# Values of a hybrid decoder layer formed by channels and turned by TensorE, in place of values formed by tokens

## The chip, the cores and the metric

The kernel runs on one core of one Trainium2 chip. The metric is device time in microseconds (us) of one execution. The engines are named as in the profile: PE (TensorE, matmuls; PEld its weight loads), DVE (VectorE), ACT (ScalarE), POOL (GpSimd), SP (which issues the DMAs).

## The reference

One decoder layer over 1024 tokens of width 1024, all in float32: an RMS norm, one combined input projection, three mixers side by side (a gated linear recurrence HGRN2 with 4 heads of 128, a sparse attention over the best 256 keys of each query, a cross-attention to 256 memory tokens), an output projection with residual, and a SwiGLU feed-forward part with residual.

```python
h = rmsnorm(x, norm_mix[layer])
hq, hf, hi, hg, sq, sk, sv, iq, ik, iw, mq = split_in(h @ w_in[layer])
o_hg = hgrn2_mix(hq, hf, hi, hg, lb[layer], hg_out_gain[layer])
o_sa = dsa_mix(sq, sk, sv, iq, ik, iw, sa_q_gain[layer], sa_k_gain[layer])
o_mem = mem_mix(mq, mem_n, w_mem_kv[layer], ...)
x = x + concat([o_hg, o_sa, o_mem]) @ w_out[layer]
a, b = split(rmsnorm(x, norm_ffn[layer]) @ w_ffn_in[layer])
x = x + (silu(a) * b) @ w_ffn_out[layer]
```

The change concerns `hi` (1024 tokens x 512, the values of the four HGRN2 heads) and `sv` (1024 x 256, the values of the sparse attention). Both are used with tokens on the partitions.

## The kernel before, in words

The normed tokens lie transposed, channels on partitions: `H[p][k][hf]` is the high (p = 0) or low (p = 1) part of channels 128k to 128k + 127 of token half `hf` (512 tokens), not yet scaled by the tokens' RMS factor. Each fp32 product is made in three passes over high and low parts (`PASSES`). The factor is applied later: `rn` holds it with tokens on partitions, `rrow` as a row over the tokens.

Most projections (`proj`, line 186) hold a 128x128 block of weights stationary and move 512 tokens; the result has channels on partitions and goes through a PSUM bank of tag `mm`. Each PSUM tag has two banks. The values need tokens on partitions, so `token_major` (lines 447 to 461) holds a block of 128 tokens stationary and moves 256 weight columns: 8 token tiles x 2 halves of the contraction x 12 matmuls (L457) into four banks (`lg`, `lg`, `sm`, `sm`), two token tiles a bank. `scaled_rows` (L463 to L467) copies them out on ACT, scaled by `rn` (8 copies, L466). There are three calls: `hgrn_v(0)` (heads 0 and 1), `sparse_values`, `hgrn_v(1)` (heads 2 and 3).

Around them run, interleaved on the engines:

- two searches for the 256th best score (`bisect`, L622): 31 bits each, one count of all keys per bit. The V search (blocks 7 and 4) counts on DVE (L646). The S search (blocks 6, 5, 3, 2) counts on ACT (L643, four counts a bit) and steps on DVE (L648, L655, L658, L638). Behind the search, the masks of the four blocks are made one by one: L668 counts, then for each block L678 on DVE, L680 on POOL, L683, L684 and L685 on DVE, L686 on POOL.
- the recurrence of each head: the projections and gates (L485, L497 to L506, sigmoids on ACT), then `hgrn_intra`: a descent over widths w = 1, 2, 4 to 64, in which PE forms products (L518, L553) and `descend` multiplies Q on DVE (L527), K on POOL (L528) and the decay on DVE (L529). `hgrn_state` then transposes the descended K (L571, copied by ACT, L572) and forms the states (L578, L594, L596). Nothing of L571 needs the values; L578 does.
- the memory attention (L697 to L724; exponentials on ACT, L704), the sparse queries and keys, and the loading and splitting of weight pages (L117 on ACT, L118 on POOL).

Every engine executes its instructions in order. That order is not the program's: the framework plans it, with its own model of times, and with tile releases placed by it, so that a change in one place moves instructions elsewhere. Once planned it is fixed.

Of the kernel before, what the change touches and what calls it, by code (L numbers as in the profile page):

```python
# [15 lines left out]
AF = mybir.ActivationFunctionType  # L16
# [26 lines left out]
def hybrid_block(ctx, tc, xT, memT, wch, wikw, wv, wkm, wvm, woa, wob, wfi, wfo,  # L43
                 vec, cst, lvl, out):
    nc = tc.nc
    V, S, G, T = nc.vector, nc.scalar, nc.gpsimd, nc.tensor
# [17 lines left out]
    def tmp(n=512):  # L64
        return tp.tile([128, n], F32, tag="tmp", name=nm("tmp"))

    def bank(tag):

        return pp.tile([128, 512], F32, tag=tag, name=nm(tag))
# [10 lines left out]
    def hs(hf):  # L80
        return slice(hf * 512, hf * 512 + 512)

    def bs(b):
        return slice(b * 128, b * 128 + 128)
# [23 lines left out]
    ident = cs[:, C_ID:C_ID + 128]  # L108
# [29 lines left out]
    PASSES = ((0, 0), (0, 1), (1, 0))  # L138
# [305 lines left out]
    Vh = [None] * 4  # L444
    heads = {}

    def token_major(g0):

        acc = [bank("lg"), bank("lg"), bank("sm"), bank("sm")]
        for g in range(2):  # L450
            w = load_page(wv[g0 + g], 4, 256)
            for tt in range(8):
                o = acc[tt // 2][:, 256 * (tt % 2):256 * (tt % 2) + 256]
                i = 0
                for pw, p in PASSES:
                    for k in range(4):
                        T.matmul(o, H[p][4 * g + k][tt // 4][:, bs(tt % 4)], w(pw, k),  # L457
                                 start=g == 0 and i == 0 and tt % 2 == 0,
                                 stop=g == 1 and i == 11 and tt % 2 == 1)
                        i += 1  # L460
        return [a.rearrange("p (t d) -> p t d", t=2) for a in acc]

    def scaled_rows(dst, acc):  # L463

        for tt in range(8):
            S.activation(dst[tt // 4][:, tt % 4, :], acc[tt // 2][:, tt % 2, :], AF.Copy,  # L466
                         scale=rn[:, tt:tt + 1])  # L467

    def hgrn_v(pair):
        ph[0] = "hg"  # L470
        Vp = [xt(10 + j, [128, 4, 256]) if pair else mt(4 + j, (128, 4, 256)) for j in range(2)]
        scaled_rows(Vp, token_major(2 * pair))
        for j in range(2):
            Vh[2 * pair + j] = lambda c, j=j: Vp[c // 4][:, c % 4, bs(j)]

# [273 lines left out]
    def sparse_values():  # L749
        ph[0] = "sap"  # L750
        sv.extend((xt(6, [128, 4, 256]), xt(7, [128, 4, 256])))
        scaled_rows(sv, token_major(4))

    def sparse_queries():
        ph[0] = "sap"
# [604 lines left out]
```

## Time and profile before

| | us |
|---|---|
| median of 3 executions (lowest, highest) | 1390.32 (1389.21, 1392.29) |
| the profiled execution | 1390.27 |
| its span | 1388.5 |
| PE, DVE, ACT, POOL busy | 1302.4, 1056.7, 692.0, 475.1 |

The span is the time between the first and the last recorded instruction; the profiled execution's own time is 1.8 us longer. A busy time counts an engine's instructions, whether or not anything waits for them, and an average over the span says nothing of a stage: the windows and the chain of waits show which engine ends last where. The feed-forward part, from about 560 us on, is untouched by the change.

### The profile page before, as it was taken

To read this page: it belongs to the slowest core of one execution; us is meant where nothing else is said; L and a number is where in the kernel's file an instruction comes from. 1 tells how busy PE (TensorE), PEld (TensorE's weight loads), DVE (VectorE), ACT (ScalarE), POOL (GpSimd) and SP (SyncE) were. 2 spreads that over 40 slices of the span, in tenths; PEclk is the share of its full clock that TensorE was granted. 3 is DMA by queue.
4 is the path that set the end of the run, shared out by engine and by line. 5 is a ranking of instruction groups with operands and counts; after the bars stand their busy time and mean duration, and the time that the engine had idled before them with its cause. 6 is when DMAs were issued, how large, how long until landed. Compare 5 with 4: busy or idle time off the path is not lost.

```text
span 1388.5 us, 22035 instructions
## 1 busy us (share of the span) xinstructions
PE 1302.4 (94%) x8072; PEld 1066.3 (77%) x8072; DVE 1056.7 (76%) x2094; ACT 692.0 (50%) x1369; POOL 475.1 (34%) x395
## 2 busy tenths in 40 slices
PE   7989999988989995999997999999999998999998
PEld 4767787668878884776885888888888886878887
DVE  8696998896469689775678787777787766696764
ACT  7555879956853243656454333333333334334442
POOL 2311033355257633424005233232332210384520
PEclk9999999999999996899998999999999999999999
DMA  6210010000010001013331322223223219754241
GB/s 236 69 39 16 28 50 16 32 32 32 31 48 31 26 26 46 2 61 125 125 108 61 114 99 105 93 92 113 99 99 107 91 54 346 238 185 154 84 145 61
DMA packets 53244, 122.19 MB, mean 88 GB/s; under 512 B 6032, under 2 KB 6160, under 8 KB 53136
## 3 DMA queue, kind: packets, MB, share of 16 engines
q1 hardware_dynamic: 52848, 120.58, 25.2%
q8 instruction: 63, 1.03, 0.3%
q14 instruction: 45, 0.37, 0.1%
q10 hardware_dynamic: 288, 0.22, 0.1%
HBM read 92.19 MB, written 28.57 MB: 87 GB/s over the span
## 4 chain that ended last, share of the span: by engine, by line
PE 59%; DVE 6%; POOL 2%; ACT 2%; issue 2%; DMA 1%; ACTq 0%; DVEq 0%; POOLq 0%
PE ff_lg L1093 17%; PE ff_rc L1093 12%; PE fo_mm L1252 4%; PE fo_sm L1252 4%; PE wo_mm L1052 3%; PE fo_lg L1252 2%; PE fo_rc L1252 2%; PE wo_sm L1052 2%; PE sap_mm L186 2%; PE hg_mm L186 2%; PE sat_sm L856 1%; PE sat_lg L830 1%; PE wo_mm L186 1%; PE sat_mm L875 1%; PE sat_rc L875 1%
## 5 line engine op out<-in xcount | busy, mean ns | idle before, releaser
L117 ACT ACTIVATE ff_whi<-ff_x 128x512 fp32r<-128x512 f32 x112 | 70.0, 629 | 125.4 <-PE ff_rc L1093 70.1
L643 ACT ACTIVATE idx_x<-idx_x,packs 128x896 int8<-128x896 f32 (+3 forms) x128 | 105.7, 826 | 41.6 <-DVE packs L638 34.9
L1093 PE MATMUL ff_lg<-wo_h,ff_whi 128*128 128x512 f32 x396 | 104.8, 391 | 2.8 <-ACT wo_h L117 2.8
L186 PE MATMUL hg_mm<-xn_h,hg_whi 128*128 128x512 f32 x384 | 96.9, 395 | 0.0
L1093 PE MATMUL ff_rc<-wo_h,ff_whi 128*128 128x512 f32 x308 | 90.5, 393 | 0.6 <-DVE wo_h L177 0.6
L1093 PE MATMUL ff_lg<-wo_x,ff_whi 128*128 128x512 f32 x308 | 84.9, 404 | 5.3 <-ACT ff_tmp L1100 4.8
L1093 PEld LDWEIGHTS ff_lg<-wo_h,ff_whi 128*128 128x128 f32 x396 | 74.6, 188 | 18.7 <-ACT wo_h L117 3.3
L118 DVE TENSOR_TENSOR ff_wlo<-ff_x,ff_whi 128x512 fp32r<-128x512 f32 x112 | 82.1, 741 | 8.7 <-ACT ff_whi L117 4.0
L186 PEld LDWEIGHTS hg_mm<-xn_h,hg_whi 128*128 128x128 f32 x384 | 70.5, 188 | 14.5 <-issue 0.7
L118 POOL TENSOR_TENSOR hg_wlo<-hg_wst,hg_whi 128x512 fp32r<-128x512 f32 x32 | 43.0, 1356 | 104.9 <-ACT hg_whi L117 79.4
L1093 PEld LDWEIGHTS ff_lg<-wo_x,ff_whi 128*128 128x128 f32 x308 | 57.6, 192 | 24.0 <-ACT ff_whi L117 7.3
L646 DVE TENSOR_SCALAR_CACHE_REDUCE idx_x<-idx_x,packs 128x1024 int8<-128x1024 f32 x64 | 68.7, 1074 | 0.9
L1093 PEld LDWEIGHTS ff_rc<-wo_h,ff_whi 128*128 128x128 f32 x308 | 58.6, 190 | 13.6 <-DVE wo_h L177 1.4
L1093 PE MATMUL ff_rc<-wo_x,ff_whi 128*128 128x512 f32 x220 | 64.3, 389 | 0.0
L1030 POOL TENSOR_TENSOR ff_x<-ff_wst 128x512 f32<-128x512 f32 x7 | 13.4, 1911 | 134.6 <-PE wo_sm L1052 71.3
L528 POOL TENSOR_TENSOR hg_x<-hg_x,hg_x 128x256 f32<-128x256 f32 x56 | 49.4, 898 | 29.0 <-PE hg_rc L518 18.7
L1093 PE MATMUL ff_lg<-wo_h,ff_wlo 128*128 128x512 f32 x198 | 55.8, 390 | 0.0
L388 DVE SCALAR_TENSOR_TENSOR idx_x<-idx_tmp,packs,idx_x 128x512 f32<-128x512 f32 (+2 forms) x70 | 46.1, 710 | 12.2 <-ACT idx_tmp L383 11.9
L118 DVE TENSOR_TENSOR fo_wlo<-fo_tmp,fo_whi 128x512 fp32r<-128x512 f32 x33 | 33.2, 1006 | 27.0 <-ACT fo_whi L117 27.0
L186 PE MATMUL hg_mm<-xn_h,hg_wlo 128*128 128x512 f32 x192 | 50.9, 397 | 0.0
L1093 PEld LDWEIGHTS ff_rc<-wo_x,ff_whi 128*128 128x128 f32 x220 | 41.3, 188 | 8.6
L118 DVE TENSOR_TENSOR fo_wlo<-fo_h,fo_whi 128x512 fp32r<-128x512 f32 x31 | 33.5, 1081 | 18.1 <-ACT fo_whi L117 18.0
(484 smaller groups left out, 3697.5 us busy)
## 6 DMA issues: line engine op xcount, KB each, us to landing
gd<-ff_m SPq DMA_DIRECT2D x77, 256.0 KB, 2.0
fo_x<-gd SPq DMA_DIRECT2D x77, 256.0 KB, 4.0
ff_x<-wfi SPq DMA_DIRECT2D x16, 512.0 KB, 3.4
ff_wst<-wfi SPq DMA_DIRECT2D x14, 512.0 KB, 3.3
ff_m<-wfi SPq DMA_DIRECT2D x14, 512.0 KB, 3.2
hg_wst<-wch SPq DMA_DIRECT2D x12, 512.0 KB, 3.3
fo_x<-wfo SPq DMA_DIRECT2D x24, 256.0 KB, 5.2
fo_h<-wfo SPq DMA_DIRECT2D x20, 256.0 KB, 4.4
```

The source lines that it names most:

```text
L117: S.activation(hi, src, AF.Copy)
L118: (eng or V).tensor_sub(lo, src, hi.bitcast(F32))
L186: T.matmul(ps[:M, :], w(pw, k), h[p][k][hf], start=i == 0, stop=i == len(order) - 1)
L388: V.scalar_tensor_tensor(sc[b][:, c0:c1], rl[:, :c1 - c0], iww[:, b, h:h + 1], sc[b][:, c0:c1], op0=ALU.mult, op1=ALU.add)
L528: G.tensor_mul(Kv[:, :, 0, :], Kv[:, :, 0, :], fr.to_broadcast([128, n, w]))
L643: S.activation(waste[S][:, :nk], sc[b], AF.Sign, bias=nf[:, j:j + 1], accum_out=ct[:, j:j + 1])
L646: eng.tensor_scalar(waste[eng][:, :nk], sc[b], fl[:, j:j + 1], None, op0=ALU.is_ge, op1=ALU.add, accum_out=ct[:, j:j + 1])
L830: T.matmul(lg[:, :c1 - c0], qst[h][b // 4][:, bs(b % 4)], kst[h][p][c][:, :c1 - c0], start=p == 0, stop=p == 1)
L875: T.matmul(po[ROWS[j], 0:128], sv[kb // 4][:, kb % 4, 128 * m + 64 * j:128 * m + 64 * j + 64], PTs[j][:, kb, :], start=kb == 0, stop=kb == ...
L1052: mm = T.matmul(ps, lhs, rhs, start=i == 0, stop=i == len(steps) - 1)
L1093: mm = T.matmul(ps, w[pw][:, bs(k)], HB[u][k][p], start=first and i == 0, stop=i == 11, skip_group_check=True)
L1252: T.matmul(banks[m], w[i][pw][:, bs(m)], b[i][p], start=first and i == 0 and n == 0, stop=i == NP - 1 and n == 2, skip_group_check=True)
```

## The change

`token_major` and `scaled_rows` go; `values(g0, dst)` takes their place in all three calls. It holds 128 weight columns stationary and moves 512 tokens: 2 contraction halves x 2 column blocks j x 2 token halves hf x 12 matmuls (in the new file still L457) into four banks of the same tags. The result has channels on partitions. Then for each of the four banks DVE multiplies it by `rrow` into an SBUF tile (L463), PE transposes four 128x128 blocks into a bank of tag `mm` (L466), and ACT copies that bank to its place (L467). The values end up where they were.

```diff
--- before.py
+++ after.py
@@ -444,32 +444,32 @@
     Vh = [None] * 4
     heads = {}
 
-    def token_major(g0):
-
-        acc = [bank("lg"), bank("lg"), bank("sm"), bank("sm")]
+    def values(g0, dst):
+
+        acc = [[bank(t), bank(t)] for t in ("lg", "sm")]
         for g in range(2):
             w = load_page(wv[g0 + g], 4, 256)
-            for tt in range(8):
-                o = acc[tt // 2][:, 256 * (tt % 2):256 * (tt % 2) + 256]
-                i = 0
-                for pw, p in PASSES:
-                    for k in range(4):
-                        T.matmul(o, H[p][4 * g + k][tt // 4][:, bs(tt % 4)], w(pw, k),
-                                 start=g == 0 and i == 0 and tt % 2 == 0,
-                                 stop=g == 1 and i == 11 and tt % 2 == 1)
-                        i += 1
-        return [a.rearrange("p (t d) -> p t d", t=2) for a in acc]
-
-    def scaled_rows(dst, acc):
-
-        for tt in range(8):
-            S.activation(dst[tt // 4][:, tt % 4, :], acc[tt // 2][:, tt % 2, :], AF.Copy,
-                         scale=rn[:, tt:tt + 1])
+            for j in range(2):
+                for hf in range(2):
+                    i = 0
+                    for pw, p in PASSES:
+                        for k in range(4):
+                            T.matmul(acc[j][hf], w(pw, k)[:, bs(j)], H[p][4 * g + k][hf],
+                                     start=g == 0 and i == 0, stop=g == 1 and i == 11)
+                            i += 1
+        for j in range(2):
+            for hf in range(2):
+                t = tmp()
+                V.tensor_mul(t, acc[j][hf], rrow[:, hs(hf)])
+                tb = bank("mm")
+                for c in range(4):
+                    T.transpose(tb[:, bs(c)], t[:, bs(c)], ident)
+                S.activation(dst[hf][:, :, bs(j)], tb.rearrange("p (a b) -> p a b", a=4), AF.Copy)
 
     def hgrn_v(pair):
         ph[0] = "hg"
         Vp = [xt(10 + j, [128, 4, 256]) if pair else mt(4 + j, (128, 4, 256)) for j in range(2)]
-        scaled_rows(Vp, token_major(2 * pair))
+        values(2 * pair, Vp)
         for j in range(2):
             Vh[2 * pair + j] = lambda c, j=j: Vp[c // 4][:, c % 4, bs(j)]
 
@@ -749,7 +749,7 @@
     def sparse_values():
         ph[0] = "sap"
         sv.extend((xt(6, [128, 4, 256]), xt(7, [128, 4, 256])))
-        scaled_rows(sv, token_major(4))
+        values(4, sv)
 
     def sparse_queries():
         ph[0] = "sap"
```

The plan of every engine's order changes with it. Three places follow; in the rows, out<-in name tiles, the numbers are the tiles' own, and `waits` names the engine (or DMA queue) whose signal an instruction waits for.

First place, behind the S search, DVE: before, from the first w = 64 multiplication (L527 of shape 128x4x64) of head 1's descent on.

```order
L527 TENSOR_TENSOR hg_x_499_2775<-hg_x_499_2775,hg_x_501_2777 128x4x64 [waits PE_49]
L678 TENSOR_SCALAR idx_x_156_809,packs<-idx_x_158_811,packs 128x512 [waits DVE_49]
L527 TENSOR_TENSOR hg_x_499_2775<-hg_x_499_2775,hg_x_501_2777 128x4x64 [waits PE_49]
L529 TENSOR_TENSOR hg_x_501_2777<-hg_x_501_2777 128x4 [waits DVE_49]
L681 TENSOR_SCALAR packs<-packs 128x1 [waits DVE_49]
L683 SCALAR_TENSOR_TENSOR idx_x_158_811<-idx_x_158_811 128x512 [waits Pool_49]
L529 TENSOR_TENSOR hg_x_501_2777<-hg_x_501_2777 128x4 [waits DVE_49]
L684 SCALAR_TENSOR_TENSOR idx_x_158_811<-idx_x_158_811,packs 128x512 [waits DVE_49]
L561 COPY hg_tot_3844<-hg_x_501_2777 128x8 [waits DVE_49]
L685 SCALAR_TENSOR_TENSOR idx_x_158_811<-idx_x_156_809,idx_x_158_811 128x512 [waits DVE_49]
L678 TENSOR_SCALAR idx_x_156_809,packs<-idx_x_157_810,packs 128x384 [waits DVE_49]
```

The two w = 64 multiplications stand around L678 of the third block, ahead of its L683. After the change, from the third block's L684 on:

```order
L684 SCALAR_TENSOR_TENSOR idx_x_158_811<-idx_x_158_811,packs 128x512 [waits DVE_49]
L527 TENSOR_TENSOR hg_x_507_2703<-hg_x_507_2703,hg_x_509_2705 128x8x32 [waits PE_49] x2
L685 SCALAR_TENSOR_TENSOR idx_x_158_811<-idx_x_156_809,idx_x_158_811 128x512 [waits DVE_49]
L529 TENSOR_TENSOR hg_x_509_2705<-hg_x_509_2705 128x8 [waits DVE_49] x2
L678 TENSOR_SCALAR idx_x_156_809,packs<-idx_x_157_810,packs 128x384 [waits DVE_49]
L681 TENSOR_SCALAR packs<-packs 128x1 [waits DVE_49]
L683 SCALAR_TENSOR_TENSOR idx_x_157_810<-idx_x_158_811 128x384 [waits Pool_49]
L684 SCALAR_TENSOR_TENSOR idx_x_157_810<-idx_x_157_810,packs,idx_x_158_811 128x384 [waits DVE_49]
L685 SCALAR_TENSOR_TENSOR idx_x_157_810<-idx_x_156_809,idx_x_157_810 128x384 [waits DVE_49]
L527 TENSOR_TENSOR hg_x_507_2703<-hg_x_507_2703,hg_x_509_2705 128x4x64 [waits PE_49] x2
L529 TENSOR_TENSOR hg_x_509_2705<-hg_x_509_2705 128x4 [waits DVE_49] x2
L561 COPY hg_tot_3700<-hg_x_509_2705 128x8 [waits DVE_49]
```

The w = 32 pair now comes behind L684 of the third block, the w = 64 pair behind L685 of the fourth.

The same place on POOL, before, from the third block's L680 on (idx_x is a block's scores, hg_wlo a weight page's low part):

```order
L680 TENSOR_SCALAR idx_x_158_811<-idx_x_158_811,packs 128x512 [waits DVE_49,Pool_49]
L118 TENSOR_TENSOR hg_wlo_4527<-hg_wst_4524,hg_whi_4526 128x512 [waits DMAHW1_49,PE_49,Activation_49]
L118 TENSOR_TENSOR hg_wlo_4531<-hg_wst_4524,hg_whi_4530 128x512 [waits PE_49,Activation_49]
L528 TENSOR_TENSOR hg_x_500_2776<-hg_x_500_2776,hg_x_501_2777 128x4x64 [waits PE_49,Pool_49]
L686 TENSOR_SCALAR idx_x_156_809<-idx_x_156_809 128x768 [waits DVE_49]
L528 TENSOR_TENSOR hg_x_500_2776<-hg_x_500_2776,hg_x_501_2777 128x4x64 [waits PE_49,Pool_49]
L680 TENSOR_SCALAR idx_x_158_811<-idx_x_157_810,packs 128x384 [waits DVE_49,Pool_49]
```

and after the change, from the same L680 on:

```order
L680 TENSOR_SCALAR idx_x_158_811<-idx_x_158_811,packs 128x512 [waits DVE_49,Pool_49]
L686 TENSOR_SCALAR idx_x_156_809<-idx_x_156_809 128x768 [waits DVE_49]
L528 TENSOR_TENSOR hg_x_508_2704<-hg_x_508_2704,hg_x_509_2705 128x8x32 [waits PE_49] x2
L680 TENSOR_SCALAR idx_x_158_811<-idx_x_157_810,packs 128x384 [waits DVE_49,Pool_49]
L686 TENSOR_SCALAR idx_x_158_811<-idx_x_158_811 128x512 [waits DVE_49]
L118 TENSOR_TENSOR hg_wlo_4373<-hg_wst_4370,hg_whi_4372 128x512 [waits DMAHW2_49,PE_49,Activation_49]
L686 TENSOR_SCALAR idx_x_157_810<-idx_x_157_810 128x384 [waits DVE_49]
L118 TENSOR_TENSOR hg_wlo_4377<-hg_wst_4370,hg_whi_4376 128x512 [waits PE_49,Activation_49]
L528 TENSOR_TENSOR hg_x_508_2704<-hg_x_508_2704,hg_x_509_2705 128x4x64 [waits PE_49,Pool_49] x2
```

The last w = 64 instruction of POOL (L528, 128x4x64) stood ahead of the fourth L680; now the pair stands behind the fourth L680, behind L686 of the last two blocks and behind another weight split.

Second place, PE at the transposes of head 1's K (L571, 128x128), before:

```order
L186 MATMUL hg_mm_4498<-xn_h_176,hg_whi_4468 128x512
L571 MATMUL hg_rc_4073<-packs,hg_x_500_2776 128x128 [waits Pool_49]
L571 MATMUL hg_rc_4073<-packs,hg_x_500_2776 128x128 x3
L186 MATMUL hg_mm_4498<-xn_h_180,hg_whi_4468 128x512
L186 MATMUL hg_mm_4498<-xn_h_184,hg_whi_4468 128x512
L571 MATMUL hg_rc_4079<-packs,hg_x_500_2776 128x128 [waits Pool_49]
L571 MATMUL hg_rc_4079<-packs,hg_x_500_2776 128x128 x3
L186 MATMUL hg_mm_4498<-xn_h_188,hg_whi_4468 128x512
L186 MATMUL hg_mm_4498<-xn_h_159,hg_wlo_4465 128x512
```

and after:

```order
L186 MATMUL hg_mm_4282<-xn_h_187,hg_wlo_4253 128x512
L553 MATMUL hg_rc_3684<-hg_x_507_2703,hg_x_508_2704 64x64 [waits DVE_49,Pool_49]
L553 MATMUL hg_rc_3684<-hg_x_507_2703,hg_x_508_2704 64x64 x3
L553 MATMUL hg_rc_3684<-hg_x_507_2703,hg_x_508_2704 64x64 [waits DVE_49,Pool_49]
L553 MATMUL hg_rc_3684<-hg_x_507_2703,hg_x_508_2704 64x64 x3
L571 MATMUL hg_rc_3857<-packs,hg_x_508_2704 128x128 [waits Activation_49,Pool_49]
L571 MATMUL hg_rc_3857<-packs,hg_x_508_2704 128x128 x3
L571 MATMUL hg_rc_3863<-packs,hg_x_508_2704 128x128 [waits Activation_49,Pool_49]
L571 MATMUL hg_rc_3863<-packs,hg_x_508_2704 128x128 x3
```

Projection matmuls (L186) stood between and behind the transposes, 39 of a pair of 48 ahead of the last four; now all 48 are done before the w = 64 products (L553), and the transposes follow these at once.

Third place, ACT in the S search, where sigmoids (L499, L500) and exponentials (L704) alternate: before,

```order
L499 ACT_TABLE_LOAD
L499 ACTIVATE hg_x_465_2284<-hg_x_466_2285 128x512
L500 ACTIVATE hg_x_466_2285<-hg_x_466_2285 128x512
L643 ACTIVATE idx_x_158_811,packs<-idx_x_155_808,packs 128x896
L643 ACTIVATE idx_x_158_811,packs<-idx_x_156_809,packs 128x768
L724 ACTIVATE mat_m_365_1631<-mat_sm_2017 128x128
L643 ACTIVATE idx_x_158_811,packs<-idx_x_158_811,packs 128x512
L715 ACTIVATE mat_m_383_1866<-mat_rc_2037 128x512
L704 ACT_TABLE_LOAD
```

and after:

```order
L704 ACT_TABLE_LOAD
L704 ACTIVATE mat_m_390_1793,mat_sm_2009<-mat_lg_2003,mat_mx_2008,packs 128x256 x2
L500 ACT_TABLE_LOAD
L500 ACTIVATE hg_x_474_2213<-hg_x_474_2213 128x512
L643 ACTIVATE idx_x_158_811,packs<-idx_x_155_808,packs 128x896
L643 ACTIVATE idx_x_158_811,packs<-idx_x_156_809,packs 128x768
L643 ACTIVATE idx_x_158_811,packs<-idx_x_158_811,packs 128x512
L724 ACTIVATE mat_m_364_1630<-mat_sm_1971 128x128
L643 ACTIVATE idx_x_158_811,packs<-idx_x_157_810,packs 128x384
L704 ACT_TABLE_LOAD
L704 ACTIVATE mat_m_390_1793,mat_sm_2035<-mat_lg_2029,mat_mx_2034,packs 128x256 x2
```

The sigmoids L499 and L500 of one half stood behind one table load; now exponentials come between them and each needs a load. In the whole program there are four more table loads than before, all four among the counts of the S search.

## Rows read from the trace of the kernel before

**Rows 1.** The page, section 1: busy time of each engine, share of the span, instructions.
```profile
PE 1302.4 (94%) x8072; PEld 1066.3 (77%) x8072; DVE 1056.7 (76%) x2094; ACT 692.0 (50%) x1369; POOL 475.1 (34%) x395
```

**Rows 2.** Chain that ended last, 380 to 520: start, length (us), what.
```profile
414.11 2.54 POOL idx_x L680
...
436.06 1.02 POOL hg_x L528
437.13 0.66 PE hg_rc L571 x4
...
439.85 1.56 PE hg_rc L578 x14
...
444.76 10.90 PE hg_mm L186 x48
455.66 0.88 PE hg_rc L612 x8
...
505.17 3.46 PE sap_mm L186 x15
508.73 0.68 DVE sap_h L811
```

**Rows 3.** Timeline of DVE: the last count of the S search taken up.
```profile
405.91 0.17 DVE L648 TENSOR_TENSOR packs<-packs 128x4 int32<-128x4 f32 x1 [1.82 <-ACT idx_x L643]
```

**Rows 4.** Waits, 154 to 406: engine, line, what released it, total us, times, longest.
```profile
DVE packs L648 <- ACT idx_x L643: 38.6, 16, 5.0
...
ACT idx_x L643 <- DVE packs L638: 34.9, 21, 6.0
```

**Rows 5.** Windows: us; busy of PE, PEld, DVE, ACT, POOL; clock; DMA.
```profile
154.00:214.00 60.00, 59.79 (x390) 52.77 (x388) 58.34 (x180) 47.82 (x114) 14.02 (x16) 1.00 0.11 36
214.00:275.00 61.00, 56.58 (x336) 43.39 (x337) 51.35 (x152) 56.54 (x131) 24.41 (x36) 1.00 0.08 27
...
414.10:437.10 23.00, 21.19 (x170) 18.59 (x168) 22.37 (x33) 7.62 (x17) 22.38 (x17) 1.00 0.11 40
...
304.00:308.00 4.00, 3.38 (x12) 3.10 (x13) 3.96 (x14) 2.26 (x6) 1.32 (x1) 0.50 0.00 0
...
441.00:508.70 67.70, 67.70 (x751) 56.46 (x750) 49.43 (x138) 20.68 (x38) 29.59 (x32) 1.00 0.11 34
508.70:558.00 49.30, 32.02 (x473) 26.26 (x471) 47.73 (x123) 20.07 (x33) 20.06 (x17) 0.69 0.10 33
```

**Rows 6.** Groups by line and form, DVE, 140 to 440: total us, mean ns.
```profile
L485 DVE TENSOR_TENSOR hg_x<-hg_mm,rrow 128x512 f32<-128x512 f32 x12 | 8.2, 682 | 1.1 <-PE hg_mm L186 1.1
```

**Rows 7.** Groups by line and form, ACT, 140 to 440.
```profile
L704 ACT ACT_TABLE_LOAD x4 | 5.1, 1283 | 0.1
...
L572 ACT ACTIVATE hg_x<-hg_rc 128x512 f32<-128x512 f32 x4 | 2.4, 588 | 0.7 <-POOL hg_x L528 0.6
...
L466 ACT ACTIVATE hg_m<-hg_lg,packs 128x256 f32<-128x256 f32 x4 | 1.7, 464 | 0.0
```

**Rows 8.** Timeline of PE in the first call: start, length (us), what.
```profile
151.70 1.12 PE L457 MATMUL hg_lg<-hg_whi,xn_h 128*128 128x256 f32 x8
152.66 0.64 PE L457 MATMUL hg_lg<-hg_wlo,xn_h 128*128 128x256 f32 x4
153.14 1.12 PE L457 MATMUL hg_lg<-hg_whi,xn_h 128*128 128x256 f32 x8
```

**Rows 9.** Timeline of POOL behind the S search.
```profile
423.95 2.66 POOL L528 TENSOR_TENSOR hg_x<-hg_x,hg_x 128x256 f32<-128x256 f32 x2
...
430.70 3.45 POOL L118 TENSOR_TENSOR hg_wlo<-hg_wst,hg_whi 128x512 fp32r<-128x512 f32 x2
...
437.06 1.24 POOL L680 TENSOR_SCALAR idx_x<-idx_x,packs 128x384 int8<-128x384 f32 x1
438.38 1.33 POOL L686 TENSOR_SCALAR idx_x<-idx_x 128x512 f32<-128x512 f32 x1
```

**Rows 10.** Waits of PE, 150 to 440, the longest kind.
```profile
PE hg_rc L518 <- DVE hg_x L527: 6.2, 6, 3.4
```

## The prediction

> **What bounds the kernel now.** I read the page first: TensorE (PE) is busy 94% of a span of 1388.5 us [rows 1], which says that most of the program is paced by matmuls but not which part of it the three changed calls lie in. So the second view is the chain of waits: from 441 us to 508.7 it is PE without a gap, then DVE (the split of the sparse keys, L811), later PE again to the end [rows 2]. Just ahead of that the chain leaves PE: it goes back over the last diagonal transposes L571, a POOL product L528 and the POOL masks L680 to the instant at which DVE takes up the last count of the S search, L648 at 405.91 [rows 2, 3]. I call that instant E. All three calls (150 to 188, 312 to 353, 388 to 424 us) lie before it or just behind it, so two questions decide: when does E come, and how long is it from E to the continuous PE stretch.
>
> Third, the waits: before E, DVE waits 38.6 us for the ACT counts, ACT waits 34.9 us for the DVE steps [rows 4]. The search is thus a ping-pong of ACT and DVE, and PE only matters to it indirectly. Fourth, the windows: in 154 to 214 DVE is busy 58.34 of 60 us, in 214 to 275 ACT 56.54 of 61; from 414.1 to 437.1 DVE 22.37 and POOL 22.38 of 23; in 441 to 508.7 PE 67.70 of 67.70; behind that DVE 47.73 of 49.3 [rows 5]. What is lost before 441 is therefore passed on: the PE stretch behind it has no idle time to give back.
>
> All sums are made against the profiled execution, 1390.27 us, which is the median of the runs shown (1390.32) within 0.05.
>
> **The change part by part.**
>
> *PE.* A call had 192 matmuls with 256 moving columns, 12 in 1.44 us (151.70 to 153.14) [rows 8], 0.120 us each, so 23.0 us. Now it has 96 with 512; the projection of the same shape runs 48 in 10.90 us [rows 2], 0.227 each, so 21.8. The 16 transposes are priced by L612, the same 128x128 form, 8 in 0.88 us [rows 2]: 1.76 a call. Net +0.56 us a call, 1.7 in all. Before E PE has waits of its own (the longest kind alone 6.2 us [rows 10]) and I take 0; the bounds are 0 and +1.7. Halving the weight loads buys nothing by itself: they go with the matmuls, and the rows price both together.
>
> The Trainium skill ("TensorE: Matmul & The Clock Gate", Part 4: PE-mode transpose) speaks against this change more strongly: it gives about 275 ns for a 128x128 transpose inside a kernel. By that figure 16 would be 4.4 us a call and the net +3.2 a call, 9.6 in three; the trace's 110 ns per transpose is what I use.
>
> *DVE.* Twelve multiplies of 128x512 out of PSUM are new; L485 is the same operation, 682 ns [rows 6]. The four of the first call, 2.7 us, come into the stretch where DVE is busy 58.34 of 60 [rows 5] and the search's own steps queue behind them: +2.7 on E. The four of the second call come where DVE waits for ACT [rows 4]: 0. The four of the third lie behind E, beside POOL's masks: 0 of their own, since POOL is the pacer there (below). Bounds for all twelve: 0 and +8.2.
>
> *ACT.* 24 copies of 128x256 at 464 ns go, 12 of 128x512 at 588 ns come [rows 7]: 11.1 less 7.1, a gain of 4.1 us. But the new order has four more table loads, 1283 ns each [rows 7], all in the part of the S search where sigmoids (L499, L500) and the exponentials of the memory attention (L704) alternate among its counts: +5.1. Of the copies, 16 gone and 8 new lie before E (7.4 and 4.7), so the net on ACT before E is +2.4. ACT waits 34.9 us for DVE in that span [rows 4], but only 4.5 of it lie in 214 to 275 [rows 5]. I take 0, since DVE is the one I have lengthened already; bounds 0 and +5.1.
>
> On the trace these loads have 0.1 us of idle time before four of them [rows 7], so their price is 1.28 each. The Trainium skill ("ScalarE: Activation LUTs", What ACT_TABLE_LOAD costs) adds a drain and puts a switch at about 2.66 us. By that the four loads would be 10.6 us instead of 5.1; no row here shows such a gap.
>
> *The order behind E*, the largest term. Before, head 1's last two descents (w = 32 and 64: L527 on DVE, L528 on POOL) were spread among the masks of the four blocks, and the last L528 ended at 437.07, 31.2 us after E [rows 2, 3]. Now DVE does its w = 64 pair only after L685 of the fourth block, and POOL its w = 64 pair after every L680 and L686. POOL was busy 22.38 of the 23.0 us from its first mask to that last L528 [rows 5], so whatever is put ahead of the last L528 delays it. That is one more pair L528 (w = 8, 2.66), one more pair L118 (3.45), the fourth L680 (1.24), L686 of the third block (1.33) [rows 9] and of the fourth (scaled from the third by its width, an estimate of 1.0): 9.7 us. Behind it PE saves something: before, 9 projection matmuls stood between L571 and L578, which began 2.72 us after L571 [rows 2]; now they are done earlier, and L578 waits only for the L571 pair and two copies L572 (0.3 + 0.1 + 2 x 0.588 [rows 7], say 1.6), 1.1 less. So +8.6 from E to the state of PE at L578, and PE then idles some 6 us before L571. Bounds: 0 (if POOL's instructions run shorter with DVE less busy beside them, or PE is late itself) and +9.7 plus what the clock takes: where PE starved at about 300 us the granted clock was 0.50 in the next 4 us [rows 5], at most 2 us lost; so +11.7.
>
> *Nothing else.* SP issues the same transfers, and up to the output projection in the same order, so no transfer is added or moved past another in the part that counts.
>
> Sum: 0 + 2.7 + 0 + 8.6 = +11.3, so **1401.6 us**.
>
> **The rivals.** A difference of 0.2% (2.8 us) is about what a measurement of this kernel can tell from no change.
>
> *Faster: the calls are shorter where they count.* PE has no idle time to speak of in 154 to 214 (59.79 of 60 [rows 5]). If matmul progress sets that part, the 23.0 against 21.8 us counts with 1.2 us in each of three calls, the transposes fall into PE's waits, ACT's lighter copies before E give another 2.7, and the masks hide the late L528: 1390.3 - 3.6 - 2.7 = 1384.0. Against it: the search waits for ACT and DVE, never for PE [rows 4], and POOL behind E is full. It decides if E comes before 403. By the Trainium skill ("TensorE: Matmul & The Clock Gate", Back-to-back issue gap) a sustained stream with 512 columns runs at 131 ns a matmul, which would make this rival much stronger (12.6 us a call); the projections here, at 227, disagree.
>
> *No difference: the order behind E costs nothing.* If POOL waited on DVE rather than set the pace from 414 to 437 (DVE is as busy, 22.37 [rows 5]), the late w = 64 pair may come with the fourth mask only a little later than before, and the first call's 2.7 us may fit into the 1.7 us that DVE has free in 154 to 214: 1390 to 1392.
>
> *Slower still: table loads and bank waits.* ACT is the fuller engine from 214 to 275. If the four loads stand on the ping-pong there, E moves 5.1 more: 1401.6 + 5.1 = 1406.7. The transposes write to the two banks that projections use; where PE stands at one until a multiply is done, one multiply a group is the price, 0.7 us, so up to 2.7 in a call.
>
> **How the numbers follow.** The forecast (E later by some us, L571 some 8 later behind it) 0.60; slower still 0.14; no difference 0.12; faster 0.14. So slower by over 0.2%: 0.74, within 0.2%: 0.12, faster: 0.14. The whole order before E is planned anew and can move E by a few us either way without any of these terms. The range runs from 1388 (the forecast's tail cut to nothing and half the gain of the first rival's copies) to 1408 (slower still with some waits at banks); the forecast's own range is 1394 to 1407. What it leaves out are the fast rival and the far side of the slow one, about 2 in 10.
>
> **What would show it.** In the profile after: 12 in 2.72 us for L457, 110 ns for each transpose, 682 for L463, 588 for L467; 15 or 16 table loads; the last L648 of the S search at 407 to 411 instead of 405.91; a wait of PE at L571 on POOL L528 of about 6 us; L578 some 41 us after E instead of 33.9; then again about 67.7 us of PE without a gap. I am wrong if E is not later than 406, if L571 has no wait, or if the stretch behind 441 is shorter than before by as much as the stretch ahead of it is longer.

## The result and the profile after

The change makes the kernel slower: 1399.64 us (median of 4 executions, 1397.66 to 1401.30) against 1391.30 for the kernel before on the same chip, a ratio of 1.0061 (95% interval 1.0045 to 1.0077), +8.3 us by the medians. The forecast was 1401.6, +11.3. The profiled execution took 1398.90 us with a span of 1397.1.

The page's first section, beside [rows 1]:

```profile
PE 1309.1 (94%) x7832; PEld 1061.0 (76%) x7832; DVE 1063.5 (76%) x2106; ACT 695.4 (50%) x1361; POOL 473.5 (34%) x395
```

PE is busy 6.7 us more and DVE 6.8; the span grew by 8.6. The average says no more than that. The chain that ended last, beside [rows 2] (start, length, what):

```profile
444.12 0.59 POOL hg_x L528
...
444.76 1.97 PE hg_rc L571 x8
446.73 2.48 PE hg_rc L578 x14
...
452.56 10.93 PE hg_mm L186 x48
463.49 0.88 PE hg_rc L612 x8
...
512.95 3.46 PE sap_mm L186 x15
...
516.50 0.68 DVE sap_h L811
```

and on DVE's timeline the last count of the S search, beside [rows 3], the instant E:

```profile
405.18 0.14 DVE L648 TENSOR_TENSOR packs<-packs 128x4 int32<-128x4 f32 x1
```

E is at 405.18, not later than before (405.91): the search takes 0.8 us longer and begins 1.5 us earlier. From E to the first transpose L571 it is 39.6 us (before 29.7), to L578 41.6 (before 33.9), to the first L612 58.3 (before 49.8). From L612 on, both kernels need the same: the projection that ends in DVE's L811 takes 3.46 us in both, and from L612 to the end of the span it is 933.6 us against 932.8. So the whole loss lies between E and L612. The waits (engine, line, releaser: us, times, longest), of PE in 150 to 450 us and of DVE and ACT in 154 to 415, beside [rows 4, 10]:

```profile
PE hg_rc L571 <- POOL hg_x L528: 6.1, 1, 6.1
PE hg_mm L466 <- DVE hg_tmp L463: 4.0, 3, 1.4
```

```profile
DVE packs L648 <- ACT idx_x L643: 19.4, 12, 4.1
...
DVE hg_x L485 <- PE hg_mm L186: 8.1, 4, 2.6
DVE hg_m L485 <- PE hg_mm L186: 4.2, 2, 2.2
```

```profile
ACT idx_x L643 <- DVE packs L638: 20.0, 13, 3.0
```

PE stands 6.1 us at L571 and waits for POOL's L528. POOL's timeline shows what came ahead of that instruction, beside [rows 9]:

```profile
420.95 2.20 POOL L680 TENSOR_SCALAR idx_x<-idx_x,packs 128x768 int8<-128x768 f32 x1 [2.18 <-DVE hg_x L529]
...
435.01 1.73 POOL L528 TENSOR_TENSOR hg_x<-hg_x,hg_x 128x256 f32<-128x256 f32 x2
436.72 1.93 POOL L680 TENSOR_SCALAR idx_x<-idx_x,packs 128x384 int8<-128x384 f32 x1
438.73 1.36 POOL L686 TENSOR_SCALAR idx_x<-idx_x 128x512 f32<-128x512 f32 x1
440.17 1.44 POOL L118 TENSOR_TENSOR hg_wlo<-hg_wst,hg_whi 128x512 fp32r<-128x512 f32 x1
442.12 0.61 POOL L686 TENSOR_SCALAR idx_x<-idx_x 128x384 f32<-128x384 f32 x1 [0.51 <-DVE idx_x L685]
442.81 1.31 POOL L118 TENSOR_TENSOR hg_wlo<-hg_wst,hg_whi 128x512 fp32r<-128x512 f32 x1
444.09 1.20 POOL L528 TENSOR_TENSOR hg_x<-hg_x,hg_x 128x256 f32<-128x256 f32 x2
```

Between the w = 32 pair (435.01) and the w = 64 pair (444.09) stand the fourth L680, the last two L686 and two weight splits, as the plan had it. The windows (us; busy of PE, PEld, DVE, ACT, POOL; granted clock; DMA), beside [rows 5]:

```profile
154.00:214.00 60.00, 58.59 (x321) 49.19 (x320) 58.44 (x182) 46.47 (x110) 14.85 (x18) 1.00 0.11 36
214.00:275.00 61.00, 54.36 (x313) 42.41 (x311) 48.33 (x146) 57.77 (x125) 22.48 (x32) 0.94 0.08 27
414.10:437.10 23.00, 19.42 (x174) 15.47 (x174) 21.56 (x33) 6.81 (x13) 20.22 (x17) 0.93 0.08 24
440.00:442.00 2.00, 0.00 (x0) 0.00 (x0) 1.97 (x3) 0.00 (x0) 1.53 (x2) 0.86 0.00 0
442.00:444.00 2.00, 0.00 (x0) 0.00 (x0) 2.00 (x4) 0.00 (x0) 1.80 (x2) 0.50 0.00 0
444.00:446.00 2.00, 1.24 (x6) 1.24 (x7) 0.70 (x3) 0.04 (x1) 1.28 (x3) 0.50 0.43 102
446.00:448.00 2.00, 2.00 (x10) 1.72 (x9) 0.00 (x0) 1.16 (x2) 0.00 (x0) 0.50 0.43 168
448.00:450.00 2.00, 2.00 (x19) 2.00 (x18) 1.25 (x4) 0.00 (x0) 0.00 (x0) 0.94 0.00 0
452.60:516.40 63.80, 63.80 (x716) 52.64 (x715) 46.60 (x130) 20.00 (x37) 26.76 (x29) 1.00 0.10 29
```

PE does nothing from 440 to 444. Its granted clock is then 0.50, the lower level of 1.2 GHz, from 442 to 448, and so the 14 matmuls L578 take 2.48 us in place of 1.56. From 452.6 on PE is busy without a gap, as it was before. The rows of prices, beside [rows 6 to 8]: PE's value matmuls, DVE's multiplies, ACT's copies and table loads.

```profile
408.27 1.98 PE L457 MATMUL hg_lg<-xn_h,hg_whi 128*128 128x512 f32 x8
410.08 1.07 PE L457 MATMUL hg_lg<-xn_h,hg_wlo 128*128 128x512 f32 x4
410.99 1.98 PE L457 MATMUL hg_sm<-xn_h,hg_whi 128*128 128x512 f32 x8
```

```profile
L704 ACT ACT_TABLE_LOAD x6 | 7.7, 1283 | 0.1
...
L463 DVE TENSOR_TENSOR hg_tmp<-hg_lg,rrow 128x512 f32<-128x512 f32 x4 | 2.7, 686 | 0.0
...
L467 ACT ACTIVATE hg_m<-hg_mm 128x512 f32<-128x512 f32 x4 | 2.2, 598 | 1.4 <-PE hg_mm L466 1.4
```

Twelve matmuls take 2.72 us (408.27 to 410.99), 227 ns each; a multiply 686 ns, a copy 598.

### The profile page after: what moved, and what is told of

It reads as the page before. It is cut to its first block, busy times and chain, and to the rows that moved or that the text cites. A ratio compares the mean times of both kernels' runs of the same rounds, so it can differ in the third digit from the quotient of the medians.

```text
span 1397.1 us, 21562 instructions
## 1 busy us (share of the span) xinstructions
PE 1309.1 (94%) x7832; PEld 1061.0 (76%) x7832; DVE 1063.5 (76%) x2106; ACT 695.4 (50%) x1361; POOL 473.5 (34%) x395
## 4 chain that ended last, share of the span: by engine, by line
PE 59%; DVE 5%; ACT 2%; issue 1%; DMA 1%; POOL 0%; ACTq 0%; DVEq 0%; POOLq 0%
PE ff_lg L1093 17%; PE ff_rc L1093 12%; PE fo_mm L1252 4%; PE fo_sm L1252 4%; PE wo_mm L1052 3%; PE fo_rc L1252 3%; PE fo_lg L1252 3%; PE wo_sm L1052 2%; PE sap_mm L186 2%; PE hg_mm L186 2%; PE sat_sm L856 1%; PE sat_lg L830 1%; PE wo_mm L186 1%; PE sat_rc L875 1%; PE sat_mm L875 1%
## 5 line engine op out<-in xcount | busy, mean ns | idle before, releaser
L186 PE MATMUL hg_mm<-xn_h,hg_whi 128*128 128x512 f32 x384 | 102.2, 410 | 0.0
L186 PEld LDWEIGHTS hg_mm<-xn_h,hg_whi 128*128 128x128 f32 x384 | 73.2, 196 | 14.8 <-issue 0.3
L118 POOL TENSOR_TENSOR hg_wlo<-hg_wst,hg_whi 128x512 fp32r<-128x512 f32 x32 | 41.6, 1314 | 108.9 <-ACT hg_whi L117 66.9
L528 POOL TENSOR_TENSOR hg_x<-hg_x,hg_x 128x256 f32<-128x256 f32 x56 | 49.6, 904 | 30.4 <-PE hg_rc L518 24.5
L186 PE MATMUL hg_mm<-xn_h,hg_wlo 128*128 128x512 f32 x192 | 52.0, 404 | 0.0
L1093 PE MATMUL ff_rc<-wo_h,ff_wlo 128*128 128x512 f32 x154 | 46.5, 395 | 0.0
```

The lines of the kernel that those rows point to most:

```text
L118: (eng or V).tensor_sub(lo, src, hi.bitcast(F32))
L186: T.matmul(ps[:M, :], w(pw, k), h[p][k][hf], start=i == 0, stop=i == len(order) - 1)
L528: G.tensor_mul(Kv[:, :, 0, :], Kv[:, :, 0, :], fr.to_broadcast([128, n, w]))
L1093: mm = T.matmul(ps, w[pw][:, bs(k)], HB[u][k][p], start=first and i == 0, stop=i == 11, skip_group_check=True)
```

## The experiments

Each kernel was timed in five rounds against the kernel before on the same chip. Besides the time, three stages of its profiled execution are given: the S search (from the first count on ACT to E), E to L571 and E to the first L612. They can be told apart because the edits leave the plan ahead of E as it is in the kernel that they start from; first_call_only and sparse_call_only have orders of their own there, and in third_call_only and first_two_calls little but the third call's own instructions differs ahead of E. Line numbers shift by the lines added; the names are those of the kernels before and after.

| kernel | ratio to before (95%) | S search, us | E to L571 | E to L612 |
|---|---|---|---|---|
| before | 1 | 251.6 | 29.7 | 49.6 |
| the change | 1.0061 (1.0045 to 1.0077) | 252.4 | 39.6 | 58.1 |
| tail_restored | 1.0031 (1.0020 to 1.0041) | 252.4 | 35.7 | 56.2 |
| tail_late_in_before | 1.0028 (1.0016 to 1.0039) | 253.2 | 34.7 | 53.2 |
| third_call_only | 1.0086 (1.0070 to 1.0102) | 253.9 | 39.7 | 59.4 |
| idle_filled | 1.0044 (1.0027 to 1.0062) | 249.9 | 41.1 | 58.4 |
| masks_last | 1.0068 (1.0048 to 1.0089) | 249.3 | 29.5 | 56.4 |
| masks_last_in_before | 1.0015 (0.9999 to 1.0032) | 251.6 | 19.6 | 48.7 |
| first_call_only | 0.9991 (0.9979 to 1.0004) | 253.9 | 13.8 | 45.5 |
| sparse_call_only | 1.0024 (1.0010 to 1.0038) | 253.9 | 29.7 | 49.5 |
| tail_staged | 1.0016 (1.0000 to 1.0031) | 249.2 | 29.7 | 55.4 |
| third_call_scaled_on_act | 1.0042 (1.0026 to 1.0059) | 249.4 | 38.6 | 56.7 |
| third_multiplies_late | 1.0085 (1.0060 to 1.0109) | 249.3 | 26.6 | 55.5 |
| first_two_calls | 0.9977 (0.9962 to 0.9991) | 249.9 | 23.4 | 49.2 |

(Here E is read to 0.1 us and L571 and L612 are the starts on PE's timeline, where the figures above are those of the chain, so the first two rows differ from them by up to 0.2.)

### The order alone, taken back and put into the kernel before

`marks` holds, for each head, width and half, the DVE and POOL instructions of `descend`; `issue_after` puts what is traced inside it behind an instruction on that engine's queue. tail_restored, in `bisect`:

```diff
+            if on_act and j == 2:
+                with tc.issue_after(marks[1, 64, 1][1]):
+                    G.tensor_scalar(sc[b], sc[b], -NEG, 0.0, op0=ALU.mult, op1=ALU.add)
...
+            if on_act and j == 3:
+                with tc.issue_after(marks[1, 64, 1][0]), tc.issue_after(marks[1, 64, 1][1]):
+                    mask(j, b)
```

> The changed kernel with one edge of order: the fourth block's mask, and the third block's L686, are issued behind head 1's w = 64 products on DVE and POOL, as they were before the change. Everything ahead of that place stays as in the changed kernel. Theory (the late w = 64 pair on POOL costs the time): the last L528 ends some 34 us after E instead of 40.1, PE's wait at L571 falls from 6.1 us to under 2, the clock stays up, and the time falls by 5 to 8 us, to 1392 to 1395. Rival (the time was lost before E or in the matmuls and transposes themselves): within 2 us of the changed kernel, 1398 to 1401.

Measured: 1395.61 us, 1.0031. PE's wait at L571 (L574 there):

```profile
PE hg_rc L574 <- POOL hg_x L530: 2.3, 1, 2.3
```

The time is down by 4 of the 8 us by the medians, below the 5 to 8 expected; the wait is not under 2 and L571 comes at 35.7. By the stage between E and L612, the one that the edge acts on, it is only 1.9 us of 8.5: the w = 64 pair is not all of it.

tail_late_in_before puts the opposite edge into the kernel before:

```diff
+            for hf in range(2):
+                for i, m in zip(marks[1, 64, hf], (lastv, last)):
+                    tc.add_manual_dep(i, m.ins.name, mybir.DependencyInfo(
+                        mybir.DependencyClass.NoSync, mybir.DependencyReason.DATA),
+                        reason="late")
```

(`lastv` and `last` are the last mask's instructions on DVE, L685, and on POOL, L686.)

> The kernel before, values by tokens, with head 1's w = 64 products queued behind the last mask on DVE and POOL, as the change's plan has them. Theory: the order alone costs what the change costs behind E, so PE waits 4 to 7 us at L571 and the time is 5 to 9 us above the kernel before, 1396 to 1400. Rival (the values' new form costs it): no difference from before, within 2 us.

Measured: 1396.21 us, 1.0028, just at the low end. PE's wait at L571 (L574 there) in 400 to 460 is shorter than the 4 to 7 us expected:

```profile
PE hg_rc L574 <- POOL hg_x L530: 2.5, 1, 2.5
```

No instruction of the values was touched, and L612 comes 3.6 us later. So the late w = 64 pair alone costs 3.6 us where the change adds 8.5 between E and L612 (taken back in the changed kernel it gave 1.9); the rest needs something else.

### One call at a time

```diff
-        scaled_rows(Vp, token_major(2 * pair))
+        if pair == 1:
+            values(2 * pair, Vp)
+        else:
+            scaled_rows(Vp, token_major(2 * pair))
```

> Only the values of heads 2 and 3 (the third call) are formed by channels. The plan up to just ahead of E is that of the kernel before, the plan behind it is that of the changed kernel. Theory: nearly the whole loss, +6 to +9 us, with E at 405 to 407 and a wait of 5 to 7 us at L571. Rival (the loss is spread over the calls, a third each): +2 to +4.

Measured: 1404.26 us, 1.0086, as much as the whole change or more (the intervals overlap), and above the +6 to +9 expected; E is at 408.3, not by 407. PE's longest wait at L571 (L596 there):

```profile
PE hg_rc L596 <- POOL hg_x L553: 3.9, 1, 3.9
```

The wait is below the 5 to 7 us expected, but E to L571 (39.7) and E to L612 (59.4) are near the change's own figures. The third call by itself makes the plan that loses, and the whole loss.

first_call_only has `pair == 0` in that line; sparse_call_only uses `values` in `sparse_values` alone.

> Only the values of heads 0 and 1 (the first call) are formed by channels. By the prediction's term the four multiplies lengthen the S search by 2.7 us: from its first count to E 254 to 255 us in place of 251.6. Rival (DVE's stretch is not what sets the search; the term is nothing): 250 to 253. Behind E the plan is near that of the kernel before, so L612 49 to 52 us after E and the time within 3 us of before for either.

> Only the values of the sparse attention (the second call) are formed by channels. Theory: the multiplies fall where DVE waits for ACT, the search stays at 250 to 253 us, the plan behind E is that of the kernel before, L612 49 to 51 us after E, time within 2 us of before. Rival (every call costs a third of the loss): +2 to +4.

Measured: for first_call_only 1388.76 us, 0.9991 (no difference can be told), with a plan of its own behind E that puts L571 at 13.8 and L612 at 45.5, earlier than expected; for sparse_call_only 1393.67, 1.0024, in the range of its rival, though with E to L612 as before (49.5). Both searches took 253.9 us, and so did that of third_call_only, whose first two calls are those of the kernel before. So the 2.3 us that the search of first_call_only is longer than that of before cannot be put down to its multiplies. In sparse_call_only the part behind L612, which the edit leaves alone, took 938.9 us in the profiled execution where before had 933.0; masks_last, which leaves it alone too, took 938.2, so single profiles differ there by as much without any edit, and whether the 0.2% of sparse_call_only is the call's is open.

first_two_calls, against the changed kernel (`token_major` and `scaled_rows` are put back):

```diff
-        values(2 * pair, Vp)
+        if pair == 0:
+            values(2 * pair, Vp)
+        else:
+            scaled_rows(Vp, token_major(2 * pair))
```

> The first two calls by channels, the third by tokens. Its plan behind E has the w = 64 products of POOL between the second and the third mask. Theory (the third call is what moves the plan behind E): L612 at 44 to 50 us after E, the S search 249 to 254, time 1387 to 1392. Rival (the cost of the calls adds up, first -1.6 and second +3.3 by their medians): 1392 to 1394.

Measured: 1386.49 us, 0.9977 (0.9962 to 0.9991): faster than both kernels, 5.0 us below before by the medians. By the stages of its profile 1.7 us of it is a shorter search, 0.4 lies between E and L612, and 3.4 behind L612 where nothing was changed; the first is no larger than what the search of one plan differs by from profile to profile (249.2 to 252.4), and behind L612 kernels that are not edited there took 931.6 to 938.9. So the gain is measured, its place is not.

### Is the idle time paid twice?

idle_filled adds 24 matmuls behind the w = 64 products, whose result nobody reads, in the place where PE idled:

```diff
+            if h == 1 and w == 64:
+                dm = bank("rc")
+                with tc.issue_after(mm.ins):
+                    for i in range(24):
+                        mm = T.matmul(dm, H[0][i % 8][0][:, bs(i % 4)], H[0][i % 8][1],
+                                      start=i == 0, stop=i == 23)
+                marks[h] = mm.ins
...
+            with tc.issue_after(marks[1]) if h == 1 else ExitStack():
                 for c in range(4):
                     T.transpose(rc[:, bs(c)], K[:, bs(4 * hf + c)], ident)
```

> The changed kernel with 24 added matmuls of 128x512 whose result nobody reads, on PE between the w = 64 products L553 and the transposes L571, where PE idled 6.1 us; they take 24 x 0.227 = 5.4. Theory (the idle time costs twice, once as idle time and again by a granted clock of 0.50 from 442 to 448): the clock stays at 1.00, the 8 transposes L571 and the 14 L578 take 2.4 us in place of 4.45, and the time falls by 1 to 2 us although PE does more. Rival (the clock does not matter, or PE is late for other reasons): the time is the same or up to 1 us longer.

PE's timeline there (L561 the added matmuls, L581 the transposes L571, L588 the states L578):

```profile
438.75 5.74 PE L561 MATMUL hg_rc<-xn_h,xn_h 128*128 128x512 f32 x24
444.33 1.03 PE L581 MATMUL hg_rc<-packs,hg_x 128*128 128x128 f32 x8
445.67 1.83 PE L588 MATMUL hg_rc<-hg_m,hg_x 128*128 128x128 f32 x14 [0.30 <-ACT hg_x L582]
447.33 0.61 PE L604 MATMUL hg_rc<-hg_m,hg_x 128*128 128x128 f32 x4
```

The granted clock stayed at 1.00 from 440 to 448, the 14 state matmuls took 1.66 us to the next instruction (445.67 to 447.33) in place of 2.44, and from L571 to L612 it was 17.3 us in place of 18.6: 1.3 us gained with 5.6 us of work added. But L571 itself came 1.5 us later after E (41.1 in place of 39.6), so L612 came no earlier (58.4 against 58.1). The time, 1398.87 (1.0044, 1.0027 to 1.0062), is not distinguishable from the change's. That the idle stretch is paid for again behind it is shown in the rows; its worth of about 1 us is too small for the times.

### Can the plan be mended with all three calls changed?

Three edges of order and one change of engine. masks_last puts all four masks behind the w = 64 products (`j >= 0` in place of `j == 3` in tail_restored's edit), masks_last_in_before does it in the kernel before.

> The changed kernel with all four masks behind the S search issued behind head 1's w = 64 products on DVE and POOL; the plan ahead of that place stays. Theory (behind E the descent of head 1, slowed by the masks on DVE and POOL, holds L571 and with it PE; PE has less left to do behind E than before the change, 8.4 us of value matmuls and 1.8 of transposes for 15.3): L571 at 20 to 28 us after E in place of 39.6, the 8 transposes L612 at 42 to 48 after E in place of 58.1 (before the change 49.6), and the time 10 to 15 us below the changed kernel, 1385 to 1390, below the kernel before too. Rival (PE itself, or the new multiplies and transposes, set the pace behind E): L612 not before 54, time 1395 or more.

> The kernel before with the same edge: all four masks behind head 1's w = 64 products. Theory: PE has only some 4 us of idle time behind E there, so L612 comes 45 to 49 us after E in place of 49.6 and the time falls by 0 to 4 us, 1388 to 1392. Rival: the edge is worth the same in both kernels, 10 us or more.

Measured: 1399.62 us (1.0068), a plain miss for the theory as put and within the numbers of its rival, and 1393.30 (1.0015, no difference), just above its range. L571 came 10 us earlier in both. In masks_last PE's timeline shows why it was worth nothing (L556 are the w = 64 products L553, L599 the outputs L596, L588 DVE's state step L585):

```profile
421.13 5.53 PE L186 MATMUL hg_mm<-xn_h,hg_whi 128*128 128x512 f32 x16 [0.49 <-ACT hg_x L467]
426.50 1.07 PE L186 MATMUL hg_mm<-xn_h,hg_wlo 128*128 128x512 f32 x4
427.50 1.15 PE L556 MATMUL hg_rc<-hg_x,hg_x 128*64 128x64 f32 x16
...
441.97 0.58 PE L599 MATMUL hg_rc<-hg_x,hg_x 128*128 128x128 f32 x2 [3.18 <-DVE hg_x L588]
```

First, PE's own queue has 20 projection matmuls ahead of the w = 64 products, so DVE waited 6.6 us for these. Second, the states of L585 then met the masks on DVE; PE waited 3.2 us for them, and the granted clock behind this wait was 0.56 in 442 to 444 and 0.50 in 444 to 448. The wait at L571 was replaced by one at L596, and L612 came at 56.4.

tail_staged gives back the old interleaving level by level:

```diff
+            if on_act:
+                m = marks[1, {0: 16, 1: 32, 2: 64, 3: 64}[j], 1]
+                with tc.issue_after(m[0]), tc.issue_after(m[1]):
+                    mask(j, b)
```

> The changed kernel with the masks behind the S search staged against head 1's descent as they were before the change: the first block's mask is issued behind the w = 16 products on DVE and POOL, the second's behind w = 32, the third's and fourth's behind w = 64. All of the change's instructions stay. Theory (the interleaving of descent and masks is what costs, the new instructions are cheap): L571 at 30 to 33 us after E (39.6 in the changed kernel, 29.7 before the change), L612 at 48 to 52 (58.1, 49.6), time 1389 to 1394. Rival (the third call's multiplies on DVE and transposes on PE hold the descent up by themselves): L571 not before 34, L612 at 53 to 56, time 1394 to 1397.

Measured: 1392.78 us, 1.0016 (1.0000 to 1.0031): at the level of before, with every instruction of the change in it. L571 is where it was before (29.7), as expected; L612 is not (55.4 in place of 48 to 52). PE's timeline (L574 is L571, L581 L578, L599 L596):

```profile
433.42 1.26 PE L574 MATMUL hg_rc<-packs,hg_x 128*128 128x128 f32 x8
437.24 1.83 PE L581 MATMUL hg_rc<-hg_m,hg_x 128*128 128x128 f32 x14 [2.57 <-ACT hg_x L575]
...
441.46 0.49 PE L599 MATMUL hg_rc<-hg_x,hg_x 128*128 128x128 f32 x2 [1.94 <-DVE packs L684]
```

and the window behind:

```profile
442.00:448.00 6.00, 5.50 (x26) 5.11 (x25) 4.31 (x10) 1.03 (x2) 2.72 (x3) 0.52 0.27 89
```

PE waited 2.6 us for ACT's copy of the transposes (ACT itself stood 4.1 us at it, behind DVE's mask step), 1.9 and 0.5 for the state steps on DVE, and ran at half clock for some 6 us. The masks that no longer hold up the descent now hold up the states. So the staged order gives back 2.8 us of the 8.5 between E and L612, and 5.8 stay. The time is at before's level all the same: in the profile the search, which lies ahead of the edge, took 249.2 us in place of the change's 252.4, and the part behind L612 2.2 us less. Whether the edge has any part in these, one profile cannot say.

third_call_scaled_on_act takes the third call's multiplies off DVE (copies before and per-token scales behind the transposes, on ACT); third_multiplies_late is tail_staged with these multiplies queued behind the w = 64 ones.

```diff
+                if g0 == 2:
+                    S.activation(t, acc[j][hf], AF.Copy)
+                else:
+                    V.tensor_mul(t, acc[j][hf], rrow[:, hs(hf)])
...
+                    for c in range(4):
+                        S.activation(dst[hf][:, c, bs(j)], tv[:, c], AF.Copy,
+                                     scale=rn[:, 4 * hf + c:4 * hf + c + 1])
```

> The changed kernel with the third call's scaling on ACT: an unscaled copy out of PSUM before the transposes and four copies of 128x128 with a per-token scale behind them, instead of the four multiplies on DVE. It takes 2.7 us off DVE where DVE and POOL are full. Theory of the multiplies: L571 2 to 4 us earlier than in the changed kernel, and the plan puts one w = 64 product ahead of the last L686, so L612 at 53 to 56 us after E and the time 1393 to 1397. Rival (POOL alone paces): L571 at 38 or later, time 1397 to 1400.

```diff
+                with tc.issue_after(marks[1, 64, 1][0]) if g0 == 2 else ExitStack():
                     V.tensor_mul(t, acc[j][hf], rrow[:, hs(hf)])
```

> As the staged kernel, and the third call's four multiplies on DVE come behind head 1's w = 64 multiplications. The descent meets nothing new. Theory: L571 at 24 to 30 us after E, L612 at 46 to 50, time 1386 to 1392, at the level of the kernel before or below it. Rival: PE is held at the transposes of the values instead, and the time is 1393 or more.

Measured: 1395.74 us (1.0042) with L571 only 1.0 us earlier, and 1400.78 (1.0085). The first lies in the range in time, but L571 is nearer to the rival: relieving DVE of 2.7 us does not speed the descent by as much (the prediction had put the third call's multiplies at 0), and PE waited 5.9 us for POOL's L528 one product earlier, at L553. The second had L571 at 26.6 but L612 at 55.5, and PE waited 9.3 us in the sparse attention for DVE's split of the keys (L254), where the change has no such wait but one of 8.6 at L172 that is 1.9 here; the part behind L612 took 939.7 us, 5.9 more than the change's. By what path the edge reaches that far I did not follow. The theory of its expectation fell.

## Why the prediction was right, point by point

- **The place.** Forecast: everything ahead of 441 us is passed on, since the PE stretch behind it is full. It was: from L612 to the end the two kernels differ by less than 1 us, and PE is busy without a gap from 452.6 to 516.4.
- **PE's term, 0.** The prices hold: 12 value matmuls in 2.72 us as forecast. Eight L612 took 0.88 us again, 110 ns each. The 275 ns that the Trainium skill gives for a transpose of bf16 in a kernel ("TensorE: Matmul & The Clock Gate", Part 4: PE-mode transpose) agree with the recorded length of one here, 272 ns on average, but one starts every 110 ns, so the prediction's sum by 275 ns each took the length of one for the spacing of many.
- **DVE's term, +2.7 on E: wrong, the step that failed.** The price was right (686 ns), the effect was not there. Five kernels that share the change's plan up to E (the change, tail_restored, idle_filled, masks_last, tail_staged) searched 252.4, 252.4, 249.9, 249.3 and 249.2 us, and two more with the same order there (third_call_scaled_on_act, third_multiplies_late) 249.4 and 249.3; three that share the plan of before (before, tail_late_in_before, masks_last_in_before) 251.6, 253.2 and 251.6. The means are 250.3 and 252.1. The step took DVE's high busy share in 154 to 214 us for a limit. Over the whole search the windows of before and of the change are (columns as above):

```profile
154.30:405.90 251.60, 230.80 (x2015) 196.05 (x2014) 198.02 (x554) 195.93 (x446) 98.89 (x107) 0.97 0.10 33
152.80:405.20 252.40, 234.59 (x1774) 190.98 (x1773) 198.72 (x561) 200.15 (x443) 96.39 (x105) 0.95 0.10 32
```

Eight multiplies of 0.69 us are new in it, yet DVE's busy time grew by 0.7 us only and its idle time stayed at 53.6 and 53.7 us. So they did not go into idle time: DVE's other instructions are recorded some 5 us shorter in sum, for a reason that no run shows, and a busy share made of such records is no fixed limit. The wait for ACT's counts did fall, from 38.6 us [rows 4] to 19.4, but others took its place: DVE waited 8.1 and 4.2 us for PE at L485, where it had waited 1.1, and the steps of the search stand behind L485 in DVE's order; the prediction had the search wait "never for PE". The sum without this term is 1398.9, and the profiled execution took 1398.90. That they meet so closely is luck: E came 0.7 us earlier, L578 7.6 later in place of 8.6, and the clock and the part behind L612 made up the rest.
- **ACT's term, 0.** The four extra table loads came, 16 in place of 12, 1283 ns each with 0.1 us idle ahead of six of them; of the drain that the Trainium skill adds ("ScalarE: Activation LUTs", What ACT_TABLE_LOAD costs) the trace again shows nothing. ACT was busy 4.2 us longer in the search and E was not later, so they were covered; ACT's waits for DVE fell from 34.9 to 20.0 us.
- **The order behind E, +8.6.** Measured +7.6 at L578 and +8.5 at L612, with a wait at L571 of 6.1 us where some 6 were forecast, and L578 41.6 us after E where 41 was. The place and the kind of cause were right (tail_late_in_before shows the order's cost without any new instruction), but the account was too simple. POOL was not full in the place: it was busy 20.22 us of 23 in 414.1 to 437.1, and waited for DVE 2.18 us at 420.95 and 0.51 at 442.12, so DVE and POOL handed the delay to each other. And the last pair is 1.9 (taken back) to 3.6 (put in) of the 8.5, not all: the whole descent runs one level later against the masks than before, which the prediction had as one more pair of POOL. Giving back the levels (tail_staged) brought L571 to where it was before, but L612 by 2.8 us only, so that the whole 8.5 comes from the order is argued and not shown. What the clock took, about 1 us, lay in the upper bound only.
- **The rivals.** The fast one named a gain of the new form that a plan behind E might let through; with the third call left as it was, it does (first_two_calls, -5.0 us). With all three calls it was outweighed. The slower one, table loads in the search, did not come.

## What to carry to other kernels

Where a scheduler plans each engine's order anew, compare the orders before comparing the prices: here the kernel with every new instruction and a staged order took the time of before within its interval, and one product pair queued behind two other chains cost 3.6 us in the kernel before. Read a busy share together with the waits of the same engine in the same stretch: an engine that was 97% busy over 60 us took in four more multiplies there without the chain that matters coming later, and its recorded busy time was no measure of how much room it had. And a change that is applied in several places should be tried place by place, since one place can lose what the others win.

## What was not expected

Kernels with the same order of instructions up to E reached it after 249.2 to 252.4 us of search from one profile to another, and began the search between 152.7 and 155.2; so a term of 2 or 3 us in this stage cannot be read from one profile, only from several kernels that share the plan. For the change's order the record shows what the two ends differ by. In all seven kernels PE waits 2.5 to 3.1 us, while it forms a head's states (L594), for the last multiply of the second call; the prediction had put that call's multiplies at 0. In the two kernels at 252.4 the granted clock then fell: it was 0.50 in 350 to 356 us in the change, 0.89 and 0.82 in 350 to 356 and 356 to 362 in tail_restored, and 1.00 in the other five. PE's wait in the change, and the windows of the change and of tail_staged:

```profile
350.36 1.22 PE L594 MATMUL hg_rc<-hg_m,hg_x 128*128 128x128 f32 x4 [3.10 <-DVE sap_tmp L463]
```

```profile
350.00:356.00 6.00, 5.64 (x26) 5.64 (x27) 3.84 (x13) 5.97 (x13) 0.92 (x1) 0.50 0.30 90
350.00:356.00 6.00, 4.36 (x39) 4.37 (x40) 4.22 (x12) 5.02 (x13) 2.20 (x2) 1.00 0.29 90
```

PE then reached the next projection 204.6 us after the first count in place of 201.4, and DVE waited for its product at L485 (1.4 us in place of none). No edit tested this by itself.

Moving the w = 64 products forward by 10 us gained nothing in either kernel, although PE had stood 6 us for them in one: the masks that were put off came back as waits for the states on DVE, with the granted clock at 0.52 from 442 to 448 in tail_staged.
